# Hybrid HGRN2 / gMLP trunk on one core: conditioning's small transfers on ScalarE's queue, a new sequence of its work, and rows of x scaled on ScalarE

## The chip, the cores and the metric

One Trainium2 chip, one core. The metric is device time in microseconds of one execution. Engines: TensorE (PE, its weight loads PEld), VectorE (DVE), ScalarE (ACT), GpSimd (POOL) and SyncE (SP), which issues most of the transfers. An engine executes its instructions in the order in which they stand in its queue.

## The reference

One layer over 2048 latent positions of width 1024, with a context of 256 positions. Cut to what the change touches:

```python
ada   = silu(c)     @ w_ada + b_ada        # (1024) @ (1024, 6144)
ada_c = silu(c_ctx) @ w_ada + b_ada
hc = modulate(rmsnorm(ctx, norm_mix), csh1, csc1)    # y * (1 + scale) + shift
... = hgrn2_gates(hc @ w_in[:, :3 * 512], ...)       # the context's final states
h  = modulate(rmsnorm(x, norm_mix), sh1, sc1)
... = token_mixers(h @ w_in, ...)                    # recurrence and spatial gating on x
x = x + g1 * (o @ w_out)
x = x + g2 * conv_ffn(modulate(rmsnorm(x, norm_ffn), sh2, sc2), ...)
return rmsnorm(x, norm_final)
```

All data are float32. The large products are made from two parts of each factor: a high part that the matmul reads at full rate and a low part that holds the rest (hi·hi, hi·lo, lo·hi).

## The kernel before, in words

The part that the change touches is the first some 400 us of the program.

**Conditioning** stands in a block whose order is written out by hand, lines 299 to 358: each engine gets its instructions in the order of the lines. `cs2` holds silu of `c` and of `c_ctx`. Of `w_ada`'s 512 columns at a time ("groups" 0 to 3: two of shifts, two of scales), each group is loaded in two 1 MB halves on SyncE's queue. For groups 0, 2 and 3 TensorE multiplies (`ada_products`, 4 k-blocks per half), the result is added to a row of `b_ada` in a tile `rows` (`load_bias`), and four small transposes and two small copies bring it into columns (`ada_columns`, `put_ada`). Group 1 is made on VectorE: `ada_sums(k0, k1)` adds two products of 128x512 for each k into `acc`, whose first partition was loaded with `b_ada`; 16 small matmuls against `ones` then make columns of it (`pz`).

The two context tiles `xc` are squared on ScalarE (`x_square`), the root is made on POOL (`rstd`), VectorE scales them in place (`x_scale`), and TensorE transposes them into four PSUM banks (`pct`). `ctx_mod(k, eng)` turns a k-block into high and low parts: VectorE applies scale and shift (line 231, into `xfl`, two buffers), ScalarE copies the high part (line 119), and the engine `eng` subtracts to get the low part (line 120). `split_w` does the same to a weight tile of 128x1024 (`whi`, `wlo`).

**Context banks.** `run_banks` goes through banks of 256 columns, 24 matmuls each, for heads' gates and values; each needs its weight split (two sets of `whi`, `wlo`; a set is free when its bank is done). The first uses weight columns 0, the second 512, the third 1024.

**The x stage.** After the hand-written block an automatic scheduler orders each engine's instructions. `pin` puts an instruction behind all that was written before it on its engine. `bg_q` holds work that is interleaved with the banks: `x_start` squares four rows of x tiles, makes the root, scales them (`x_scale`), and `x_first` transposes them per k and calls `x_mod` (the same three steps as `ctx_mod`, 128x512); then the next four. Low parts alternate: POOL for even k, VectorE for odd k. `x_second` does the second half of x in four groups of two, 256 columns at a time, with 6 us planned between loading, scaling and use, and writes the parts to DRAM.

Small transfers: the six rows of `vr` (norm gains and the like) are issued by ScalarE; the rows of `b_ada` by SyncE, between the large loads.

Of the kernel before, what the change touches and what calls it, by code (L numbers as in the profile page):

```python
# [13 lines left out]
AF = mybir.ActivationFunctionType  # L14
ALU = mybir.AluOpType
# [4 lines left out]
D = 1024  # L20
# [4 lines left out]
CTX = 256  # L25
HW = 512
# [46 lines left out]
def tile_trunk(ctx, tc, x, c, cx, c_ctx, w_ada, b_ada, norm_mix, norm_ffn, w_in, hg_norm, sgu_g, sgu_b,  # L73
               w_sp, b_sp, w_out, w_up, conv_w, conv_b, w_down, norm_final, masks, out):
    nc = tc.nc
    V, S, G, T = nc.vector, nc.scalar, nc.gpsimd, Tensor(nc.tensor)
    ld = nc.sync.dma_start
# [31 lines left out]
    def rstd(pool, ss, n, scale, bias=EPS, keep=lambda i: i):  # L109

        r = pool.tile([P, 8], F32, tag="rs", name="rs")
        keep(G.tensor_scalar(out=r[:, :n], in0=ss, scalar1=scale, scalar2=bias, op0=ALU.mult, op1=ALU.add))  # L112
        r2 = pool.tile([P, 8], F32, tag="rs2", name="rs2")
        G.tensor_tensor(out=r2[:, :n], in0=r[:, :n], in1=mhalf[:, :n], op=ALU.pow)  # L114
        return r2
# [61 lines left out]
    with es1:  # L177
# [21 lines left out]
        def load_raw(key):  # L199
            raw = raw_tile().rearrange("p (k c) -> p k c", c=P)  # L200
            ld(raw, w_in[:, key[0]:key[0] + P].rearrange("(k p) c -> p k c", p=P))
            w_raw[key] = raw
# [16 lines left out]
                jk = pm.tile([P, D], BF16, tag="acc", name="xjk")  # L219
                keep(S.activation(jk, xt, AF.Square, accum_out=ss[:, i0 + i:i0 + i + 1]))  # L220

        def x_scale(xs, ss, keep=pin):

            r = rstd(pm, ss[:, :len(xs)], len(xs), 1.0 / D, keep=keep)
            for i, xt in enumerate(xs):
                keep(V.tensor_scalar(out=xt, in0=xt, scalar1=r[:, i:i + 1], scalar2=None, op0=ALU.mult))

        def x_mod(pt, which, k, hi, lo, n, eng):

# [21 lines left out]
        def load_ada(g, qs=(0, 1)):  # L251

            for q in (qs,) if isinstance(qs, int) else qs:
                t = wa[g // 2][:, 4 * (g % 2) + 2 * q:4 * (g % 2) + 2 * q + 2, :]
                wts[g, q] = t.rearrange("p a (b e) -> p (a b) e", e=512)
                ld(wts[g, q], wv[:, 4 * q:4 * q + 4, g * 512:(g + 1) * 512])

        def load_bias(g, tag):
            rows[g] = pm.tile([2, 512], F32, tag=tag, name="rows", bufs=2)
            ld(rows[g], b_ada[0:1, g * 512:(g + 1) * 512].broadcast_to([2, 512]))  # L260

        def ada_products(g, q):
            if q == 0:
                pa[g] = bank("pj")
            for k in range(4 * q, 4 * q + 4):
                T.matmul(pa[g][:2, :], cs2[:, k, :], wts[g, q][:, k % 4, :], start=(k == 0), stop=(k == 7))

        def ada_columns(g):
            V.tensor_add(rows[g], rows[g], pa.pop(g)[:2, :])
            pv = bank("pj")  # L270
            for j in range(4):
                T.transpose(pv[:, 2 * j:2 * j + 2], rows[g][:, j * P:(j + 1) * P], ident[:2, :2])
            put_ada(g, [pv[:, w:8:2] for w in range(2)])

        def ada_sums(k0, k1):
            for k in range(k0, k1):
                for w in range(2):
                    V.scalar_tensor_tensor(out=acc[:, w, :], in0=wts[1, k // 4][:, k % 4, :], scalar=cs2[:, k, w:w + 1],
                                           in1=acc[:, w, :], op0=ALU.mult, op1=ALU.add)
# [13 lines left out]
        def ctx_mod(k, eng):  # L293
            x_mod(pct[k // 2][:, (k % 2) * 256:(k % 2) * 256 + 256], 1, k, chl[:, k, :], cll[:, k, :], CTX, eng)
# [4 lines left out]
        with tc.manual_schedule():  # L299
            load_ada(2)  # L300
            for i in range(2):
                ld(xc[i], cx[0][i * P:(i + 1) * P, :])
            vr = pm.tile([50, P], F32, tag="gu", name="vr", bufs=2)
            for a, n, r0 in ((norm_mix[0], 8, 0), (norm_ffn[0], 8, 8), (hg_norm[0], 4, 16), (sgu_g[0], 4, 20),
                             (sgu_b[0], 4, 24), (conv_b[0], 22, 28)):
                S.dma_start(vr[r0:r0 + n, :], a.rearrange("(r p) -> r p", p=P))
            load_bias(2, "ot")
            for q in range(2):
                load_ada(0, q)
                load_ada(1, q)  # L310
            load_bias(0, "ot")
            for w in range(2):
                ld(acc[0:1, w, :], b_ada[0:1, 512:1024])
            load_bias(3, "vv")
            load_ada(3)
            load_raw((0, CTX))
            S.activation(sg, cc, AF.Sigmoid)
            V.tensor_mul(cs2.rearrange("p k w -> p w k"), cc, sg)
            ss = x_sums()
            x_square(xc, ss, keep=lambda i: i)  # L320
            ada_products(2, 0)
            pv = bank("sc")
            T.transpose(pv[:, :50], vr, ident[:50, :50])
            V.tensor_copy(vec, pv[:, :50])
            ada_products(2, 1)
            ada_columns(2)
            x_scale(xc, ss, keep=lambda i: i)
            ada_sums(0, 4)
            ada_products(0, 0)
            for k in range(NK):  # L330
                for i in range(2):
                    o = (k % 2) * 256 + i * P
                    T.transpose(pct[k // 2][:, o:o + P], xc[i][:, k * P:(k + 1) * P], ident)
            load_raw((HW, CTX))
            ada_products(0, 1)
            ada_columns(0)
            ada_sums(4, 5)
            for k in range(4):
                ctx_mod(k, G)
                if k == 1:  # L340
                    ada_sums(5, 6)
            ada_products(3, 0)
            load_raw((2 * HW, CTX))
            for i in range(4):
                ld(xg[i], x_rows[i])
            ada_sums(6, 8)
            nxt[0, CTX] = split_w((0, CTX), G)
            ada_products(3, 1)
            pz = bank("pj")
            for w in range(2):  # L350
                for j in range(4):
                    o = 2 * (4 * w + j)
                    T.matmul(pz[:, o:o + 2], acc[:, w, j * P:(j + 1) * P], ones[:, :2], start=True, stop=True)
            ada_columns(3)
            put_ada(1, [pz[:, 8 * w:8 * w + 8:2] for w in range(2)])
            for k in range(4, NK):
                ctx_mod(k, V)
            nxt[HW, CTX] = split_w((HW, CTX), V)
        xl = p1.tile([P, NK, TH], F32R, tag="xl", name="xl", align_bytes=AL)
        xh = p1.tile([P, NK, TH], F32R, tag="xh", name="xh", align_bytes=AL)  # L360

        def x_first(g0, xs):
            for k in range(NK):
                pt = bank("mi")
                for i in range(4):
                    pin(T.transpose(pt[:, i * P:(i + 1) * P], xs[i][:, k * P:(k + 1) * P], ident))
                sl = slice(g0 * P, g0 * P + 512)
                x_mod(pt, 0, k, xh[:, k, sl], xl[:, k, sl], 512, V if k % 2 else G)
                if k % 2:
                    yield 1.6  # L370

# [1234 lines left out]
```

## Time and profile before

| | us |
|---|---|
| median of 3 runs | 2584.08 |
| lowest, highest | 2579.35, 2584.96 |
| profiled execution, its own time | 2583.23 |
| its span, first to last instruction | 2581.3 |
| TensorE busy / VectorE / POOL / ScalarE | 2503.6 / 1634.9 / 1052.7 / 905.0 |
| mean granted TensorE clock | 0.992 |

A line of the timeline reads: start, duration, engine, line, operation, output<-inputs, shapes, count, and in brackets how long the engine stood idle before it and what ended that. "ACTq" and "SPq" are the issues of transfers by ScalarE and SyncE. A row of the busy time by stretches gives the stretch, its length, each engine's busy time with its count of instructions, the granted TensorE clock (1.00 is full), the share of the DMA engines, and GB/s. "L231" is line 231 of the kernel before.

### The profile page before, as it was taken

How to read it: one execution, taken by the hardware profiler on the slowest of the kernel's cores; microseconds unless marked ns; L12 is line 12 of the kernel's file. 1: busy time of each engine (PE TensorE's matmuls, PEld its weight loads, DVE VectorE, ACT ScalarE, POOL GpSimd, SP SyncE). 2: the span in 40 equal slices, each digit the busy share in tenths (PEclk: the TensorE clock that was granted, in tenths of full speed). 3: DMA queues.
4: the chain of work that ended last, by engine and by line, in shares of the span. 5: the costliest groups of instructions: out<-in, count | busy, mean ns of one | idle time of the engine just before them, and what ended most of it. 6: DMA issues, size and time to landing. Idle time of an engine off the chain costs nothing. (4 is left out here: it accounts for less than half of the span.)

```text
span 2581.3 us, 32786 instructions
## 1 busy us (share of the span) xinstructions
PE 2503.6 (97%) x12123; PEld 2066.2 (80%) x12123; DVE 1634.9 (63%) x2174; ACT 905.0 (35%) x1524; POOL 1052.7 (41%) x871
## 2 busy tenths in 40 slices
PE   7999999999999998999999999999999999999997
PEld 4787887888888887788788888788788888888886
DVE  5867784644555666466898778599999983212212
ACT  2554334333434332344433333333333332111111
POOL 1344232232243243002687887877877810000000
PEclk8999999999999999999999999999999999999999
DMA  8355445561022124668722222732222364313221
GB/s 286 105 193 163 145 123 196 184 209 58 30 86 82 43 84 163 212 208 273 243 88 95 77 92 89 268 125 90 88 89 89 101 204 128 114 45 114 73 90 67
DMA packets 282492, 336.42 MB, mean 130 GB/s; under 512 B 31057, under 2 KB 214089, under 8 KB 278621
## 3 DMA queue, kind: packets, MB, share of 16 engines
q1 hardware_dynamic: 279076, 333.59, 39.2%
q8 instruction: 96, 1.57, 0.2%
q10 hardware_dynamic: 3257, 0.75, 0.1%
q14 instruction: 63, 0.52, 0.1%
HBM read 236.69 MB, written 97.59 MB: 129 GB/s over the span
## 5 line engine op out<-in xcount | busy, mean ns | idle before, releaser
L1281 DVE SCALAR_TENSOR_TENSOR dn<-gp,taps,dn 128x1024 f32<-128x1024 f32 x352 | 448.0, 1279 | 20.6 <-ACT dn L1278 17.3
L120 POOL TENSOR_TENSOR Al<-raw,Ah 128x512 fp32r<-128x512 f32 x264 | 344.8, 1314 | 96.2 <-ACT Ah L119 88.4
L65 PE MATMUL pj<-xh,whi 128*128 128x512 f32 x896 | 364.9, 408 | 0.5 <-ACT xh L119 0.5
L65 PE MATMUL pj<-xl,whi 128*128 128x512 f32 x896 | 351.9, 393 | 1.8 <-DVE xl L120 1.1
L65 PE MATMUL pj<-xh,wlo 128*128 128x512 f32 x896 | 352.2, 393 | 1.0 <-DVE wlo L120 1.0
L65 PE MATMUL up<-xah,Al 128*128 128x512 f32 x704 | 275.8, 392 | 2.3 <-POOL Al L120 2.3
L65 PE MATMUL up<-xah,Ah 128*128 128x512 f32 x704 | 276.3, 393 | 1.7 <-ACT Ah L119 1.7
L65 PE MATMUL up<-yl,Ah 128*128 128x512 f32 x704 | 274.3, 390 | 3.2 <-DMA yl<-yd 3.1
L112 POOL TENSOR_SCALAR rs<-ss 128x1 f32<-128x1 f32 (+1 forms) x24 | 7.1, 297 | 642.0 <-DVE xt L1516 323.3
L119 ACT CAST Ah<-raw 128x512 fp32r<-128x512 f32 x265 | 161.1, 618 | 299.2 <-PE up L65 249.4
L120 DVE TENSOR_TENSOR ml<-mr,mh 128x512 fp32r<-128x512 f32 x85 | 58.7, 690 | 299.7 <-ACT mh L119 299.7
L120 POOL TENSOR_TENSOR wlo<-raw,whi 128x1024 fp32r<-128x1024 f32 x56 | 140.8, 2514 | 230.9 <-ACT whi L119 215.6
L65 PE MATMUL up<-yh,Ah 128*128 128x512 f32 x528 | 208.1, 395 | 0.0
L65 PE MATMUL up<-yh,Al 128*128 128x512 f32 x528 | 206.9, 392 | 0.0
L65 PE MATMUL up<-xal,Ah 128*128 128x512 f32 x528 | 205.5, 389 | 0.0
L65 PEld LDWEIGHTS pj<-xh,wlo 128*128 128x128 f32 x896 | 169.0, 189 | 37.3 <-DVE wlo L120 1.7
L65 PEld LDWEIGHTS pj<-xh,whi 128*128 128x128 f32 x896 | 169.6, 189 | 34.3 <-issue 3.5
L65 PEld LDWEIGHTS pj<-xl,whi 128*128 128x128 f32 x896 | 169.6, 189 | 33.5 <-DVE xl L120 2.1
L65 PE MATMUL dn<-wo,o 128*128 128x512 f32 x768 | 184.9, 397 | 3.7 <-DMA wo<-wo_d 2.2
L65 PE MATMUL dn<-wh,ml 128*128 128x512 f32 x480 | 186.8, 389 | 0.0
L65 PE MATMUL dn<-wl,mh 128*128 128x512 f32 x480 | 186.8, 389 | 0.0
L65 PE MATMUL dn<-wh,mh 128*128 128x512 f32 x480 | 186.7, 389 | 0.0
(307 smaller groups left out, 4941.2 us busy)
## 6 DMA issues: line engine op xcount, KB each, us to landing
raw<-in_w_up_dram SPq DMA_DIRECT2D x88, 512.0 KB
raw<-in_w_in_dram SPq DMA_DIRECT2D x68, 512.0 KB
mr<-m SPq DMA_DIRECT2D x85, 256.0 KB
raw<-in_w_ada_dram SPq DMA_DIRECT2D x32, 512.0 KB
m<-cv SPq DMA_DIRECT2D x22, 544.0 KB
m<-cv SPq DMA_DIRECT2D x22, 480.0 KB
xt<-in_w_down_dram SPq DMA_DIRECT2D x19, 512.0 KB
wa<-in_w_ada_dram SPq DMA_DIRECT2D x8, 1024.0 KB
```

Source lines behind the costliest of these rows:

```text
L65: return self.engine.matmul(out, lhsT, rhs, **kw)
L112: keep(G.tensor_scalar(out=r[:, :n], in0=ss, scalar1=scale, scalar2=bias, op0=ALU.mult, op1=ALU.add))
L119: keep(S.copy(hi, raw))
L120: (eng or G).tensor_sub(lo, raw, hi.bitcast(F32))
L1281: V.scalar_tensor_tensor(out=cr, in0=gt[:, t // 3:t // 3 + RH, t % 3:t % 3 + GW], scalar=taps[:, t * NF + f:t * NF + f + 1], in1=cr, op0=A ...
```

## The change

Four things change.

1. The rows of `b_ada` (three of `rows`, two of `acc`) are issued by ScalarE, behind the rows of `vr`, all of them ahead of the sigmoid on ScalarE. In the text SyncE's large loads now come first.
2. Conditioning's sequence is new: the addition of `b_ada` is a step of its own (`ada_rows`); the first half of group 0 comes before the columns of group 2; ten of the sums follow, then the transposes, group 0's second half and columns, both halves of group 3, the other six sums, and then the context's parts; `split_w` of the first two weights runs on POOL and stands ahead of parts 0 and 2; parts 0 to 3 have their low part on VectorE, 4 and 6 on POOL, 5 and 7 on VectorE.
3. `x_scale` scales rows of x on ScalarE (Identity with a scale per partition). The context's two tiles are still scaled on VectorE.
4. In `x_first` all low parts are made on POOL.

```diff
-        def x_scale(xs, ss, keep=pin):
+        def x_scale(xs, ss):
-            r = rstd(pm, ss[:, :len(xs)], len(xs), 1.0 / D, keep=keep)
+            r = rstd(pm, ss[:, :len(xs)], len(xs), 1.0 / D, keep=pin)
             for i, xt in enumerate(xs):
-                keep(V.tensor_scalar(out=xt, in0=xt, scalar1=r[:, i:i + 1], scalar2=None, op0=ALU.mult))
+                pin(S.activation(xt, xt, AF.Identity, scale=r[:, i:i + 1]))
...
         def load_bias(g, tag):
             rows[g] = pm.tile([2, 512], F32, tag=tag, name="rows", bufs=2)
-            ld(rows[g], b_ada[0:1, g * 512:(g + 1) * 512].broadcast_to([2, 512]))
+            S.dma_start(rows[g], b_ada[0:1, g * 512:(g + 1) * 512].broadcast_to([2, 512]))
...
+        def ada_rows(g):
+            V.tensor_add(rows[g], rows[g], pa.pop(g)[:2, :])
+
         def ada_columns(g):
-            V.tensor_add(rows[g], rows[g], pa.pop(g)[:2, :])
             pv = bank("pj")
...
             load_ada(2)
             for i in range(2):
                 ld(xc[i], cx[0][i * P:(i + 1) * P, :])
+            for q in range(2):
+                load_ada(0, q)
+                load_ada(1, q)
+            load_ada(3)
+            load_raw((0, CTX))
             vr = pm.tile([50, P], F32, tag="gu", name="vr", bufs=2)
...
                 S.dma_start(vr[r0:r0 + n, :], a.rearrange("(r p) -> r p", p=P))
-            load_bias(2, "ot")
-            for q in range(2):
-                load_ada(0, q)
-                load_ada(1, q)
-            load_bias(0, "ot")
+            for g, tag in ((2, "ot"), (0, "ot"), (3, "vv")):
+                load_bias(g, tag)
             for w in range(2):
-                ld(acc[0:1, w, :], b_ada[0:1, 512:1024])
-            load_bias(3, "vv")
-            load_ada(3)
-            load_raw((0, CTX))
+                S.dma_start(acc[0:1, w, :], b_ada[0:1, 512:1024])
             S.activation(sg, cc, AF.Sigmoid)
...
             ada_products(2, 1)
+            ada_rows(2)
+            r = rstd(pm, ss[:, :2], 2, 1.0 / D)
+            for i in range(2):
+                V.tensor_scalar(out=xc[i], in0=xc[i], scalar1=r[:, i:i + 1], scalar2=None, op0=ALU.mult)
+            ada_products(0, 0)
             ada_columns(2)
-            x_scale(xc, ss, keep=lambda i: i)
-            ada_sums(0, 4)
-            ada_products(0, 0)
+            ada_sums(0, 5)
...
             load_raw((HW, CTX))
-            ada_products(0, 1)
-            ada_columns(0)
-            ada_sums(4, 5)
-            for k in range(4):
-                ctx_mod(k, G)
-                if k == 1:
-                    ada_sums(5, 6)
-            ada_products(3, 0)
             load_raw((2 * HW, CTX))
             for i in range(4):
                 ld(xg[i], x_rows[i])
-            ada_sums(6, 8)
+            ada_products(0, 1)
+            ada_rows(0)
+            ada_columns(0)
+            ada_products(3, 0)
+            ada_sums(5, 8)
+            ada_products(3, 1)
             nxt[0, CTX] = split_w((0, CTX), G)
-            ada_products(3, 1)
+            ctx_mod(0, V)
+            ctx_mod(1, V)
+            nxt[HW, CTX] = split_w((HW, CTX), G)
+            ctx_mod(2, V)
+            ctx_mod(3, V)
+            ada_rows(3)
             pz = bank("pj")
...
+            put_ada(1, [pz[:, 8 * w:8 * w + 8:2] for w in range(2)])
             ada_columns(3)
-            put_ada(1, [pz[:, 8 * w:8 * w + 8:2] for w in range(2)])
             for k in range(4, NK):
-                ctx_mod(k, V)
-            nxt[HW, CTX] = split_w((HW, CTX), V)
+                ctx_mod(k, V if k % 2 else G)
...
-                x_mod(pt, 0, k, xh[:, k, sl], xl[:, k, sl], 512, V if k % 2 else G)
+                x_mod(pt, 0, k, xh[:, k, sl], xl[:, k, sl], 512, G)
```

## The prediction

> **What bounds the kernel now.** I read the page's head first, then the busy time by stretches, then the timeline of the first 90 us, then the waits of the DMA queue's own engine.
>
> ```profile
> span 2581.3 us, 32786 instructions
> PE 2503.6 (97%) x12123; PEld 2066.2 (80%) x12123; DVE 1634.9 (63%) x2174; ACT 905.0 (35%) x1524; POOL 1052.7 (41%) x871
> ...
> core 0: us, PE busy (x) PEld busy (x) DVE busy (x) ACT busy (x) POOL busy (x), PEclk, DMA share, GB/s
> 7.00:43.50 36.50, 29.81 (x93) 10.27 (x93) 19.88 (x30) 4.87 (x9) 7.84 (x7) 0.93 1.04 380
> 43.50:55.70 12.20, 10.88 (x50) 9.60 (x51) 6.44 (x14) 6.24 (x12) 0.00 (x0) 0.66 0.34 110
> 64.70:87.00 22.30, 19.00 (x126) 15.72 (x125) 20.69 (x30) 13.00 (x24) 12.68 (x7) 1.00 0.33 95
> 87.00:105.00 18.00, 16.24 (x91) 12.43 (x90) 16.79 (x30) 7.61 (x15) 5.64 (x4) 1.00 0.26 88
> 105.00:400.00 295.00, 286.61 (x1576) 241.65 (x1576) 216.16 (x340) 125.54 (x203) 107.57 (x82) 0.99 0.49 155
> ```
>
> TensorE is busy for 97% of the span, and the change takes no matmul out. It can win or lose only where TensorE stands idle, or runs at half clock, up to about 400 us: conditioning (to 43.5), the first context banks (to 55.7), and the stage that normalises x (to 105), where VectorE is busy for 20.69 of 22.30 us while TensorE loses 3.3. After 105 us the idle is 8.4 of 295. Now the order inside conditioning:
>
> ```profile
> 6.98 5.45 PE L65 MATMUL pj<-wa,cs 128*2 128x512 f32 x8 [6.98 <-DMA wa<-in_w_ada_dram]
> 12.55 3.60 PE L65 MATMUL pj<-wa,cs 128*2 128x512 f32 x8
> 22.59 5.39 DVE L278 SCALAR_TENSOR_TENSOR acc<-wa,cs,acc 128x512 f32<-128x512 f32 x8 [3.68 <-DMA acc<-in_b_ada_dram]
> 27.90 0.67 DVE L269 TENSOR_TENSOR rows<-rows,pj 2x512 f32<-2x512 f32 x1
> ...
> 29.07 0.23 DVE L285 COPY s<-pj 128x4 f32<-128x4 f32 x2 [0.50 <-PE pj L69]
> ...
> 34.40 5.71 DVE L278 SCALAR_TENSOR_TENSOR acc<-wa,cs,acc 128x512 f32<-128x512 f32 x4
> 36.11 2.78 POOL L120 TENSOR_TENSOR wlo<-raw,whi 128x1024 fp32r<-128x1024 f32 x1
> 39.55 3.54 PE L65 MATMUL pj<-ones,acc 128*128 128x2 f32 x16 [3.56 <-POOL wlo L120]
> 43.54 0.58 PE L65 MATMUL pj<-ch,whi 128*128 128x256 f32 x1
> 44.12 0.55 DVE L231 TENSOR_SCALAR xfl<-mi,a,s 128x256 f32<-128x256 f32 x1
> 49.19 0.43 DVE L120 TENSOR_TENSOR cl<-xfl,ch 128x256 fp32r<-128x256 f32 x1 [0.47 <-ACT ch L119]
> 51.42 0.39 PE L65 MATMUL pj<-ch,wlo 128*128 128x256 f32 x1 [0.76 <-DVE wlo L120]
> ```
>
> VectorE's sums for group 1 (line 278) wait at 22.59 for a 2 KB row of b_ada that stood behind the megabyte loads on SyncE's queue. They end at 34.40 + 5.71 = 40.1, and TensorE's context banks start behind them, at 43.54. The first bank crawls behind parts 4 to 7 of the context, which end at 49.62. The second waits for its weight's low part until 51.42.
>
> **Part 1, conditioning.** One more reading of the timeline is needed here, of what POOL and VectorE do to each other:
>
> ```profile
> 118.82 2.48 POOL L120 TENSOR_TENSOR wlo<-raw,whi 128x1024 fp32r<-128x1024 f32 x1 [1.21 <-ACT whi L119]
> 118.98 2.60 DVE L469 TENSOR_TENSOR cS<-cS,tot 128x256 f32<-128x256 f32 x1
> 121.70 0.42 DVE L469 TENSOR_TENSOR cS<-cS,tot 128x256 f32<-128x256 f32 x1
> ```
>
> A VectorE piece over two SBUF tiles that meets one of POOL's lasts until POOL is done (2.60 us instead of 0.42).
>
> The row of b_ada comes early, so the sums can start when VectorE comes to them. In the new order that is after the columns of group 2, which TensorE makes only after the first half of group 0. That half has 8 matmuls like the 3.60 us row: 12.55 + 3.60 + 3.60 = 19.75, and the columns follow the rows by 29.30 - 28.57 = 0.73 today, which gives 20.5. Ten sums at 5.39 / 8 = 0.67 end at 27.2, and the rows of group 0 follow; today they start at 27.90, with eight sums done and not ten. The other six start at about 28.7 and end at 32.7 clean. Here POOL's low part of the first weight falls into them; today four sums beside such a piece took 5.71 and not 2.7, so 35.7 if it costs as much. Then four context parts wholly on VectorE: today four take 49.62 - 44.12 = 5.5, so 38.2 to 41.2. The second weight's low part now runs on POOL beside them; it costs nothing, or up to the 2.4 us of such a piece on POOL (2.48 at 118.82). So 38.2 to 43.6, and with 0.67 for the rows of group 3 and some 0.5 for their transposes the first bank starts at 39.4 to 44.8 against 43.54. Parts 4 to 7 alternate POOL and VectorE: 5.3 instead of 6.1 us, since one engine's low part overlaps the other's next part. The first bank's end moves by -4.9 to +0.5 us. I take -2.3, the middle, because both collisions have a row but neither is certain to hit in full. The second bank no longer waits for its low part; that 1.3 us is hidden by the next paragraph's chain.
>
> The clock is the second cost in this stretch.
>
> ```profile
> 36.00:38.00 2.00, 0.00 (x0) 1.00 1.01 408
> 40.00:42.00 2.00, 2.00 (x11) 0.50 0.84 235
> ```
>
> TensorE idle from 36 had half its clock by 40. In the new order it stands idle while VectorE does the four context parts, so the first bank starts at half clock again. I book no change. The Trainium skill, page "TensorE: Matmul & The Clock Gate", section "Part 1: The HAM clock gate (the "warmup" mystery)", says that an idle window of about 3.4 us halves the clock and that a busy one restores it. The halving after 36 agrees; by that rule a longer wait ahead of the first bank would cost up to one more such window at half rate, 1.7 us by an estimate from that page, and the sum would be nearer to zero.
>
> **Part 2, rows of x on ScalarE.**
>
> ```profile
> 58.40 1.06 ACT L220 ACTIVATE xjk<-xg 128x1024 bf16<-128x1024 f32 x1
> 59.99 1.06 POOL L114 TENSOR_TENSOR rs<-rs,mhalf 128x4 f32<-128x4 f32 x1
> 61.09 2.74 DVE L226 TENSOR_SCALAR xg<-xg,rs 128x1024 f32<-128x1024 f32 x4 [0.91 <-POOL rs L114]
> 63.88 0.76 PE L69 MATMUL mi<-ident,xg 128*128 128x128 f32 x5 [0.33 <-DVE xg L226]
> 66.41 3.38 POOL L120 TENSOR_TENSOR xl<-xfl,xh 128x512 fp32r<-128x512 f32 x1 [5.36 <-ACT xh L119]
> 67.59 0.68 DVE L120 TENSOR_TENSOR xl<-xfl,xh 128x512 fp32r<-128x512 f32 x1
> 71.37 1.29 POOL L120 TENSOR_TENSOR xl<-xfl,xh 128x512 fp32r<-128x512 f32 x1 [1.58 <-ACT xh L119]
> ```
>
> Squares of x's first four rows, POOL's root and the scaling are one chain, and TensorE stands at its end (63.88, waiting for xg). The squares sit on ScalarE behind the first bank's gates, so the chain moves with that bank: -2.3. The trace has no scaling on ScalarE; the nearest row is the square over the same 128x1024, 1.06 us. Four make 4.24 in place of 2.74, so this group's transposes end 1.5 us later in the chain. What waits behind the scaling on ScalarE is the next weight's cast; in exchange VectorE reaches that weight's low part 2.74 sooner, so I count no more than the 1.5. Net at this barrier: -2.3 + 1.5 = -0.8, from -3.4 to +2.0. The chain is thus the wait that takes the place of the old one: most of the gain of conditioning ends here.
>
> **Part 3, low parts of x on POOL.** Of 16 low parts eight move from VectorE (0.68) to POOL (1.29 clean, 3.38 when VectorE's own pieces come between). VectorE is rid of 8 x 0.68 = 5.4 and, with the two groups' scaling, 5.5 us more in a stage where it binds. TensorE's idle there is 3.3 + 1.8 = 5.1 us, which is the ceiling of the gain. Against it stands that POOL's extra 8 x 1.29 = 10.3 us hold VectorE: as the piece at 118.98 shows. If half of POOL's 10.3 us held VectorE, half of the 10.9 would be left. I take a quarter of the ceiling, -1.3: half of the relief is left, and of the waits that it could shorten about half hang on ScalarE's casts too. The ends are -4 (nearly the ceiling) and +4 (each of the two groups' last parts, now one behind the other on POOL, late by 2 us).
>
> **Part 4, the second half of x** (four groups of two rows between 105 and 400 us): eight scalings leave VectorE, eight come to ScalarE, 43% busy there. Its pieces have 6 us of planned distance to their users. I take 0, from -1.5 to +2.
>
> Sum: -0.8 - 1.3 + 0 = -2.1 us. The profiled execution took 2583.23 (2581.3 of span and 1.9 around it), 0.85 below the median of 2584.08. From the median: **2582.0**. The terms' ends add to -8.9 and +8.
>
> **The rivals.**
>
> A, the gain holds: TensorE has other banks to run while ScalarE scales, and the collisions of part 1 miss. Then -4.9 from conditioning and -2.5 from the x stage: 2576.7, about 2577. For it: VectorE's load in 64.7 to 87. Against: 58.40 to 63.88 is a chain that no faster VectorE shortens.
>
> B, slower: ScalarE's queue holds up the sigmoid.
>
> ```profile
> SPq L302 <- DMA vr<-in_norm_ffn_dram: 0.2, 1, 0.2
> ...
> 2.70 0.30 ACTq L306 DMA_DIRECT2D vr<-in_conv_b_dram  x1
> 3.29 1.28 ACT L317 ACT_TABLE_LOAD   x1 [3.29 <-DMA cc<-in_c_ctx_dram]
> 4.84 0.17 DVE L318 TENSOR_TENSOR cs<-cc,sg 128x16 f32<-128x16 f32 x1 [4.84 <-ACT sg L317]
> 12.09 1.06 ACT L220 ACTIVATE xjk<-raw 128x1024 bf16<-128x1024 f32 x1 [0.18 <-DMA raw<-in_ctx_dram]
> ```
>
> Six issues of about 0.3 us become eleven, ahead of the sigmoid: cs at 4.84 + 1.5 = 6.4, still under the 6.98 at which the first weights land, so hidden with 0.6 to spare. But the first row matters: the load of ctx (line 302) waited for an unrelated row of vr to land before it could be issued. If one of the five new issues waits like that for a big load, everything on ScalarE stands behind it, the sigmoid first, then all products. From a landing at about 8 us on it costs time; if it is the second ctx tile's (12.09), cs comes at 12.09 + 0.5 + 1.28 + 0.4 = 14.3, 7.3 us behind 6.98: 2582 + 7.3, about 2589.5.
>
> C, slower: POOL becomes the bound of the x stage. If the low parts all take 3.38, eight need 27 us where the first group's stretch has 22.3 and the second's 18: some 5 to 9 us on 2582: about 2589.
>
> D, the transfers don't overtake, and the row of b_ada lands at 22.59 as now. Ten sums then end at 29.3 and the rows of group 0 come 2.1 us late: 2582 + 2.1, about 2584. The Trainium skill, page "DMA: Bandwidth & Descriptors", section "Issuing engines are not separate DMA queues", says that another issuing engine saves only the issue time, since all run on the same 16 engines. No row here shows a small ScalarE transfer among large ones.
>
> **How the numbers follow.** A measurement of this kernel tells about 0.2% (5.2 us) from no change; its three runs span 5.6 us. The forecast, 2582, has 0.40, D 0.07: within 0.2%, 0.47. A has 0.30: faster. B has 0.15 and C 0.08: slower, 0.23. The range reaches from 2572 (the terms' low ends with the whole of A's first term, -10.4, and a little for the order of later work) to 2592 (the high ends, +8, and B and C).
>
> **What would show it.** Right: acc lands well before 20 us, sums start near 20.5 and end by 36, the second bank follows the first without a wait for wlo, and the transposes of xg wait for ScalarE's scaling instead, near 63. POOL's low parts average over 1.3 us. Wrong: sums still starting at 22.6 (D); the sigmoid after 7 us with a DMA issue just ahead of it (B); xg's first transposes before 60 us, with the stretch to 105 shorter by over 4 us (A); a row "PE waits for POOL xl" of several us (C). A difference that arises after 400 us would refute the whole account, since nothing of the change lies there.

## The result, and the profile after

| | before | after |
|---|---|---|
| median, us (5 runs each) | 2582.16 | 2592.78 |
| lowest, highest | 2579.35, 2584.96 | 2589.64, 2596.15 |
| ratio after/before, 95% interval | | 1.0039 [1.0025, 1.0053] |
| span of the profiled execution | 2581.3 | 2589.2 |

The change made the kernel slower by 10 us. (The prediction started from the median of the first three runs of before, 2584.08; with five it is 2582.16.) The head of the page after, and the busy time by the stretches that the prediction showed:

```profile
span 2589.2 us, 32777 instructions
PE 2507.6 (97%) x12123; PEld 2068.5 (80%) x12123; DVE 1616.4 (62%) x2151; ACT 920.7 (36%) x1540; POOL 1060.4 (41%) x878
```

```profile
7.00:43.50 36.50, 30.14 (x89) 8.54 (x89) 21.05 (x33) 7.01 (x12) 5.67 (x4) 0.93 1.04 371
43.50:55.70 12.20, 9.95 (x68) 9.67 (x69) 6.44 (x15) 6.06 (x14) 1.48 (x2) 0.79 0.36 121
64.70:87.00 22.30, 17.41 (x112) 14.50 (x111) 10.55 (x11) 17.81 (x30) 15.86 (x11) 0.98 0.19 57
87.00:105.00 18.00, 15.26 (x85) 11.76 (x83) 12.22 (x17) 7.31 (x16) 8.62 (x6) 0.93 0.34 110
```

VectorE was relieved as the change says: in 64.7 to 87 it is busy for 10.55 us instead of 20.69. TensorE, the engine that counts, did less there, 17.41 us instead of 19.00, and in the next stretch ran at a clock of 0.93 instead of 1.00. An engine that looked like the bound was freed, and TensorE gained nothing by it.

Where the time goes is read by following the same matmul through the traces. Each number is the start of that matmul against the kernel before, in us (positive is later); "hi·hi 16" is the 16th product of x's high part with a weight's high part, eight to a bank. The columns are the kernel after and four kernels of the experiments below.

| matmul (its start before) | after | conditioning alone | x stage alone | low parts alone | second half alone |
|---|---|---|---|---|---|
| first product of conditioning (6.98) | +2.1 | +2.3 | +0.2 | +0.2 | +0.2 |
| first context bank (43.54) | +2.0 | +1.7 | -0.5 | -1.4 | -0.1 |
| third context bank (55.65) | -2.9 | -1.8 | -0.5 | -1.4 | -1.6 |
| hi·hi 8 (83.21) | -2.1 | +1.9 | -2.7 | -2.3 | -1.6 |
| hi·hi 16 (97.41) | +6.0 | +7.5 | +5.3 | +5.7 | -1.6 |
| hi·hi 80 (169.13) | +4.6 | +5.9 | +3.8 | +5.4 | -2.8 |
| hi·hi 128 (214.23) | +8.1 | +5.2 | +10.1 | +5.7 | +3.5 |
| end (2581.35) | +7.9 | +0.4 | +9.1 | +4.7 | +0.3 |

Up to 115 us "second half alone" has the instructions of the kernel before in the same order on every engine, and still stands 1.6 us ahead at 56 us: single executions differ by that much, and what is smaller is not read from one trace. The medians decide on totals.

So the kernel after starts 2 us late, is 3 us ahead at the third context bank, loses 8 us between hi·hi 8 and 16 (83 to 103 us), and 3.5 us between hi·hi 80 and 128. After 215 us nothing is added in these traces.

**The start.** Timeline of the kernel after, ScalarE, VectorE and TensorE:

```profile
3.06 0.88 ACTq L260 DMA_DIRECT2D rows<-in_b_ada_dram  x3
5.43 1.84 ACTq L317 DMA_DIRECT2D acc<-in_b_ada_dram  x2
7.30 1.28 ACT L318 ACT_TABLE_LOAD   x1 [7.30 <-DMA rows<-in_b_ada_dram]
8.60 0.22 ACT L318 ACTIVATE sg<-cc 128x16 f32<-128x16 f32 x1
...
8.84 0.18 DVE L319 TENSOR_TENSOR cs<-cc,sg 128x16 f32<-128x16 f32 x1 [8.84 <-DMA wa<-in_w_ada_dram]
...
9.08 4.42 PE L65 MATMUL pj<-wa,cs 128*2 128x512 f32 x5 [9.08 <-DVE cs L319]
```

The three issues of `rows` end at 3.94; the two of `acc` take 0.23 us each and yet stretch from 5.43 to 7.27. ScalarE's queue stood still twice, and the sigmoid behind it came at 8.60. The trace keeps, with each issue, the semaphore that it waits for. The first issue of `acc` waits for number 106, and the transfer that signals 106 is the row of `vr` that ScalarE issued at 2.00; the second waits for number 100, signalled by the row of `vr` issued at 2.71. The program gives the same few semaphore numbers to one transfer after another, so an issue stands until an unrelated small row has landed, here until 5.4 and 7.0 us.

**The x stage.** The same view at 79 to 98 us:

```profile
79.25 2.53 POOL L120 TENSOR_TENSOR xl<-xfl,xh 128x512 fp32r<-128x512 f32 x2 [1.18 <-ACT xh L119]
81.86 0.19 POOL L112 TENSOR_SCALAR rs<-xss 128x4 f32<-128x4 f32 x1
82.14 1.01 POOL L114 TENSOR_TENSOR rs<-rs,mhalf 128x4 f32<-128x4 f32 x1
83.11 2.35 POOL L120 TENSOR_TENSOR wlo<-raw,whi 128x1024 fp32r<-128x1024 f32 x1
...
83.18 4.27 ACT L226 ACTIVATE xk<-xk,rs 128x1024 f32<-128x1024 f32 x4 [2.53 <-POOL rs L114]
...
85.52 0.39 PE L65 MATMUL pj<-ch,wlo 128*128 128x256 f32 x1 [2.72 <-POOL wlo L120]
...
90.48 1.53 DVE L231 TENSOR_SCALAR xfl<-mi,a,s 128x512 f32<-128x512 f32 x2 [11.57 <-PE mi L69]
...
97.03 0.50 PE L65 MATMUL pj<-xl,whi 128*128 128x512 f32 x1 [1.23 <-POOL xl L120]
```

On POOL one queue holds the low parts of x, then the root for the next four rows, then the eighth weight's low part (`wlo`). TensorE has run out of other banks and waits 2.72 us for the last of these, ScalarE waits for the middle one, and VectorE, relieved, stands idle for 11.57 us. In the kernel before, the same low part of the eighth weight stood ahead of the root on POOL:

```profile
77.00 2.38 POOL L120 TENSOR_TENSOR wlo<-raw,whi 128x1024 fp32r<-128x1024 f32 x1
...
81.58 1.06 POOL L114 TENSOR_TENSOR rs<-rs,mhalf 128x4 f32<-128x4 f32 x1
...
83.80 2.74 DVE L226 TENSOR_SCALAR xk<-xk,rs 128x1024 f32<-128x1024 f32 x4
```

What the wait costs beyond itself is in the busy time by stretches, after first and then before:

```profile
82.00:84.00 2.00, 0.80 (x4) 0.51 (x4) 0.00 (x0) 0.82 (x1) 1.92 (x3) 1.00 0.00 0
84.00:86.00 2.00, 0.48 (x4) 0.48 (x5) 0.00 (x0) 2.00 (x3) 1.46 (x1) 1.00 0.00 0
86.00:88.00 2.00, 2.00 (x13) 2.00 (x12) 0.00 (x0) 2.00 (x4) 0.00 (x0) 0.55 0.62 178
88.00:90.00 2.00, 2.00 (x13) 2.00 (x13) 0.00 (x0) 0.18 (x1) 0.00 (x0) 0.59 0.28 85
```

```profile
82.00:86.00 4.00, 3.72 (x22) 2.84 (x22) 3.31 (x6) 1.38 (x3) 0.65 (x1) 1.00 0.11 32
86.00:90.00 4.00, 3.99 (x35) 3.69 (x33) 2.51 (x5) 1.50 (x4) 1.28 (x1) 1.00 0.02 4
```

In these 8 us TensorE before works 7.71 us at full clock. After, it works 0.80 + 0.48, and then 2.00 x 0.55 + 2.00 x 0.59: 3.6 us of full clock, 4.1 less. Of that, 1.7 us (2.00 x 0.45 + 2.00 x 0.41) is the clock alone. The rest of the 8 us follows in the second group, where TensorE waits for `xl` on POOL four times between 93 and 103 us, 2.6 us in all; what makes the last 1.4 us was not separated.

**The second half of x** (timeline after, 175 to 184 us):

```profile
175.72 2.19 ACT L226 ACTIVATE xk<-xk,rs 128x1024 f32<-128x1024 f32 x2 [1.28 <-POOL rs L114]
...
179.72 1.04 ACT L119 CAST whi<-raw 128x1024 fp32r<-128x1024 f32 x1
...
181.15 2.33 POOL L120 TENSOR_TENSOR wlo<-raw,whi 128x1024 fp32r<-128x1024 f32 x1
...
183.53 0.39 PE L65 MATMUL pj<-ch,wlo 128*128 128x256 f32 x1 [2.22 <-POOL wlo L120]
```

ScalarE waits for POOL's root with the scaling at the head of its queue; the next weight's cast stands behind it (and behind a table load and an activation that before came after the cast) and ends at 180.8, and its low part on POOL at 183.5. Before, the low part was done at 173.4, 3.3 us ahead of its first use:

```profile
169.78 1.05 ACT L119 CAST whi<-raw 128x1024 fp32r<-128x1024 f32 x1 [0.67 <-PE pj L65]
170.91 2.47 POOL L120 TENSOR_TENSOR wlo<-raw,whi 128x1024 fp32r<-128x1024 f32 x1 [0.58 <-ACT whi L119]
...
176.69 0.28 PE L65 MATMUL pj<-ch,wlo 128*128 128x256 f32 x1
```

### The profile page after: what moved, and what is told of

It is laid out like the page before. It is cut to its first block, busy times and chain, and to the rows that moved or that the text cites. A ratio compares the mean times of both kernels' runs of the same rounds, so it can differ in the third digit from the quotient of the medians.

```text
span 2589.2 us, 32777 instructions
## 1 busy us (share of the span) xinstructions
PE 2507.6 (97%) x12123; PEld 2068.5 (80%) x12123; DVE 1616.4 (62%) x2151; ACT 920.7 (36%) x1540; POOL 1060.4 (41%) x878
```

## The experiments

Ratios are to the kernel before, from runs on the same chip, with 95% intervals. Expectations speak of "x banks" 79, 95 and 127 and mean single hi·hi products counted from 0; their "second x bank (97.4 us)" is the row "hi·hi 16" above.

### One part taken back

Scaling of x's rows on VectorE again, the rest as after:

```
-                pin(S.activation(xt, xt, AF.Identity, scale=r[:, i:i + 1]))
+                pin(V.tensor_scalar(out=xt, in0=xt, scalar1=r[:, i:i + 1], scalar2=None, op0=ALU.mult))
```

> The changed kernel with rows of x scaled on VectorE again; all else as changed. Theory S (ScalarE's scaling costs the time: 4.27 us against 2.74 for a group of four rows, and the second group's transposes wait for it at half clock): 5 to 8 us come back, about 2586, and the second group's first xfl starts near 87 instead of 90.5. Theory P (POOL's queue costs it: root and the eighth weight's low part stand behind eight low parts of x): at most 2 us come back, about 2591, and the wait for that low part, 2.7 us at 85.5, stays.

1.0039 [1.0027, 1.0052]: nothing comes back. That is the total of theory P, but the wait that P names is gone from the trace, and another stands there: VectorE's four scalings now meet POOL's low part of the eighth weight, take 4.81 us, and TensorE waits 3.81 us for them, so that hi·hi 16 stands at +10.8. The loss of the second half, in turn, is gone (+10.2 at hi·hi 80, +9.5 at 128).

Low parts of the first half alternating again:

```
-                x_mod(pt, 0, k, xh[:, k, sl], xl[:, k, sl], 512, G)
+                x_mod(pt, 0, k, xh[:, k, sl], xl[:, k, sl], 512, V if k % 2 else G)
```

> The changed kernel with the low parts of x's first half alternating between POOL and VectorE again; all else as changed. Theory P (POOL's queue): 5 to 8 us come back, about 2586, the 2.7 us wait of TensorE near 85 goes, and the half clock behind it. Theory S (ScalarE's scaling): at most 2 us come back, about 2591.

1.0034 [1.0022, 1.0045]. In the trace hi·hi 16 stands 2.3 us behind the kernel before instead of 6.0, so that loss is gone, but between hi·hi 80 and 96 it loses 4.5 us (from +1.8 to +6.3), and the total is within the uncertainty of the kernel after. The 5 to 8 us that theory P promised did not come back.

Both taken back, which leaves the new conditioning alone:

> The changed kernel with both reverted, so only the new conditioning and ScalarE's transfers are left. If the x stage (scaling and low parts together) holds the loss: 2580 to 2584, equal to before within 2 us, though its first context bank starts about 2 us later than before's 43.5. If conditioning with the sigmoid behind ScalarE's transfers holds it: 2588 to 2593.

1.0014 [1.0005, 1.0022], between the two totals that were expected. Alone it loses, too, although its third bank is 1.8 us early: 3.7 us up to hi·hi 8, for which see below, and 5.6 us from there to hi·hi 16, where the scaling meets POOL's low part of the eighth weight as in the first run:

```profile
85.94 2.34 POOL L120 TENSOR_TENSOR wlo<-raw,whi 128x1024 fp32r<-128x1024 f32 x1
86.00 4.81 DVE L226 TENSOR_SCALAR xk<-xk,rs 128x1024 f32<-128x1024 f32 x4 [1.18 <-POOL rs L114]
...
88.97 0.45 PE L69 MATMUL mi<-ident,xk 128*128 128x128 f32 x1 [3.26 <-DVE xk L226]
```

The x stage alone (the kernel before with both edits of the x stage):

> The kernel before with only the x stage changed (rows of x scaled on ScalarE, low parts of the first half on POOL), conditioning untouched. If the x stage holds the loss: 2589 to 2593. If conditioning holds it: 2581 to 2585.

1.0039 [1.0027, 1.0052]: the whole loss, without conditioning. Its timeline shows the 2.71 us wait for the eighth weight's low part and the 2.22 us wait of the second half, as after.

The sigmoid and `cs2` put ahead of the five b_ada transfers, the rest as after:

```
+            S.activation(sg, cc, AF.Sigmoid)
+            V.tensor_mul(cs2.rearrange("p k w -> p w k"), cc, sg)
             for g, tag in ((2, "ot"), (0, "ot"), (3, "vv")):
                 load_bias(g, tag)
...
-            S.activation(sg, cc, AF.Sigmoid)
-            V.tensor_mul(cs2.rearrange("p k w -> p w k"), cc, sg)
```

> The changed kernel with the sigmoid of c and the product cs2 placed ahead of the five b_ada transfers on ScalarE's queue. Theory (the loss is made in the x stage; the late sigmoid is a small matter of its own): cs2 back at about 4.9 us, first product at 7.0 instead of 9.1, first context bank 1 to 2 us earlier than in the changed kernel (45.5), but the wait for the eighth weight's low part and those for xl in the second group remain, so at the second x bank at most 2 us of the 8 come back: 2591, ratio 1.003 to 1.004. Rival (the late sigmoid shifts the whole chain and so makes the collisions): the x stage falls back into step, 2584 or less.

1.0029 [1.0018, 1.0039]. The first product is back at 6.9 us, 1.4 us of the 6.0 come back at hi·hi 16, and the total is near the theory's. The waits that the theory names do not stay where they were, though: at 82.03 TensorE waits 2.17 us for the scaled rows and not for the eighth weight's low part, and at 95.19 it waits 2.50 us for VectorE's `xfl`.

### The stall at 85 us, and the second half

The eighth weight's low part on VectorE:

```
-            split(hi, lo, raw, eng or (V if w_n[0] < 8 or w_n[0] < 20 and w_n[0] % 2 else G))
+            split(hi, lo, raw, eng or (V if w_n[0] < 9 or w_n[0] < 20 and w_n[0] % 2 else G))
```

> The changed kernel with the eighth weight's low part on VectorE instead of POOL, nothing else. Theory (the stall at 85.5 us is POOL's queue: that weight's low part stands behind the serial low parts of x and the root, TensorE waits 2.72 us and then runs 3 us at half clock): the wait shrinks to under 1 us, the second x bank comes 3 to 5 us earlier than in the changed kernel (103.4 us), the total is 2588 to 2590. Rival (the stall is set by ScalarE's scaling or by the second group's xl on POOL, and would only move): the wait reappears at xk or xl, second x bank within 1.5 us of the changed kernel's, 2592 to 2593.

1.0038 [1.0025, 1.0052]; hi·hi 16 at +6.7. Timeline:

```profile
85.09 4.27 ACT L226 ACTIVATE xk<-xk,rs 128x1024 f32<-128x1024 f32 x4 [3.41 <-POOL rs L114]
...
86.29 0.33 PE L69 MATMUL mi<-ident,xk 128*128 128x128 f32 x1 [2.44 <-ACT xk L226]
```

The rival holds in the trace: the wait of 2.72 us for `wlo` became one of 2.44 us for the scaled rows, which wait for POOL's root. The total, 2591.6, lies between the two expected, no different from the kernel after's.

The second half of x scaled on VectorE, the first half on ScalarE, the rest as after:

> The changed kernel with the rows of the second half of x (four groups of two) scaled on VectorE again; the first half's on ScalarE as changed. Theory (two scalings of 1.1 us on ScalarE, which also wait for POOL's root, stand ahead of the next weight's cast, so that its low part reaches TensorE late at 183.5 us, 2.2 us of idle and a lower clock behind it): no wait for wlo near 183, the 3.5 us between the x banks 79 and 127 come back, 2588 to 2590. Rival (that loss belongs to the order of later work, shifted by what came before): the loss of 3 to 4 us between those banks remains, 2592 to 2593.

1.0033 [1.0022, 1.0045], 2590.4 us. The step of 3.5 us between hi·hi 80 and 128 is gone from the trace (+7.1 to +6.4, no wait for `wlo` near 183 us). The ratio falls by 0.0006, some 1.5 us, which cannot be told from nothing. So what makes this step is shown; what it is worth in the total is not.

### Each edit of the x stage alone, on the kernel before

> The kernel before with one thing changed: the 16 low parts of the first half of x all on POOL. Theory (POOL's queue makes the loss at the second x bank: the low parts stand one behind the other, the root of the second four rows and the eighth weight's low part behind them): the second x bank comes 5 to 8 us later than before (97.4 us), total 2586 to 2591. Rival (the prediction's step: VectorE is relieved where it binds): second x bank 1 to 4 us earlier, total 2578 to 2581.

1.0024 [1.0014, 1.0035]; 8.0 us lost between hi·hi 8 and 16. Timeline, and busy time by stretches:

```profile
81.61 1.01 POOL L114 TENSOR_TENSOR rs<-rs,mhalf 128x4 f32<-128x4 f32 x1
82.59 2.34 POOL L120 TENSOR_TENSOR wlo<-raw,whi 128x1024 fp32r<-128x1024 f32 x1
...
82.65 4.81 DVE L226 TENSOR_SCALAR xk<-xk,rs 128x1024 f32<-128x1024 f32 x4 [3.74 <-POOL rs L114]
...
85.62 0.45 PE L69 MATMUL mi<-ident,xk 128*128 128x128 f32 x1 [3.59 <-DVE xk L226]
```

```profile
82.00:86.00 4.00, 0.41 (x3) 0.41 (x3) 3.35 (x2) 0.00 (x0) 2.93 (x2) 0.84 0.00 0
86.00:90.00 4.00, 4.00 (x21) 4.00 (x20) 1.94 (x4) 0.00 (x0) 0.00 (x0) 0.50 0.45 131
```

Four scalings that met POOL's low part took 4.81 us, not 2.74, and TensorE stood nearly still for 4 us and then ran at half clock for 4 more. The theory holds at hi·hi 16 and in the total.

> The kernel before with one thing changed: the rows of the second half of x scaled on ScalarE. Theory (the scaling stands ahead of the next weight's cast on ScalarE while it waits for POOL's root): nothing before 160 us; between the x banks 79 and 95 (169 to 186 us) 3 to 5 us lost, with a wait of TensorE for wlo of about 2 us; total 2585 to 2588. Rival (the prediction's step: six microseconds of planned distance cover it): within 2 us of the kernel before, 2580 to 2584.

1.0023 [1.0014, 1.0032]. The same wait of 2.22 us for `wlo` (at 177.23), a clock of 0.72 in the 6 us behind it, and 5.0 us lost between hi·hi 80 and 96. The prediction's "0" for this part is refuted.

> The kernel before with one thing changed: both groups of the first half of x scaled on ScalarE, low parts alternating as before. Theory (with POOL not serial, ScalarE's scaling is cheap here): first transposes of x 1.3 us later, as in the kernel with the x stage alone, second x bank 0 to 2 us later, total 2581 to 2584. Rival (ScalarE's scaling holds up the casts in the second group by 4.3 us): second x bank 4 us or more later, 2586 to 2588.

1.0021 [1.0012, 1.0031], 2587.3 us. Hi·hi 16 stands 1.7 us late, as the theory says, but the total is the rival's. The trace puts 2.4 us before 120 us and 3 us in the feed-forward part after 1000 us, where the change has no instruction; where this part's loss arises stays open.

Then the low parts alone once more, with the eighth weight's low part on VectorE (the edit as above):

> The kernel before with the 16 low parts of the first half of x on POOL (as in the run with the low parts alone, 1.0024) and the eighth weight's low part on VectorE instead of POOL. In the run with the low parts alone VectorE's scaling of the second four rows took 4.81 us instead of 2.74, beside POOL's low part of that weight, and TensorE waited 3.59 us for it. Theory (half of the loss is that collision, the other half that TensorE has run out of other banks by then): the scaling takes 2.7 to 3.0 us, the wait at the transposes of xk shrinks to 1 to 2 us, total 2583 to 2586. Rival (the place of that weight does not matter, the serial low parts of the second group make the loss): second x bank still 5 us or more behind the kernel before, total 2587 to 2589.

1.0020 [1.0011, 1.0030], hi·hi 16 at +6.1. Busy time by stretches:

```profile
86.00:90.00 4.00, 3.81 (x21) 3.52 (x21) 3.24 (x5) 0.54 (x2) 0.00 (x0) 0.60 0.26 78
...
94.00:98.00 4.00, 2.02 (x11) 1.39 (x9) 3.93 (x7) 2.44 (x5) 1.91 (x2) 1.00 0.00 0
98.00:102.00 4.00, 3.63 (x13) 2.94 (x14) 4.00 (x7) 1.24 (x2) 2.71 (x2) 0.68 0.54 178
```

The collision is gone (the scaling takes 2.74 us, TensorE waits 1.52 us for it), but the loss stays: a second gap of 2.34 us ends at 98.37, with a second fall of the clock. TensorE waits there for VectorE's `xfl`, which starts at 97.51 behind other work: VectorE is busy for 3.93 of the 4 us before 98. It had come late to that work, after waiting 1.55 us for POOL's `xl` before another `xfl`, and two of its pieces met POOL's low parts (1.13 and 1.40 us; such pieces take 0.43 alone). At hi·hi 16 the rival holds, and the total is just under its range: the loss does not hang on this one collision. How much of it comes of the low parts standing one behind the other on POOL, and how much of the other order of VectorE's work, is not separated.

The second half on ScalarE (against the run with that alone) with 3 us between squares and scaling:

```
                 x_square(xs, ss)
+                yield 3.0
                 x_scale(xs, ss, on_act=True)
-                yield 6.0
+                yield 3.0
```

> The kernel before with the rows of the second half of x scaled on ScalarE (as in the run with that alone, 1.0023), and 3 us of planned distance put between the squares and the scaling (taken from the 6 us behind it), so that the scheduler puts the next weight's cast ahead of the scaling on ScalarE. Theory (the loss is that cast standing behind a scaling that waits for POOL's root): no wait of TensorE for wlo near 177 us, total 2581 to 2585. Rival (ScalarE's 1.1 us a row against VectorE's 0.75 is itself the loss, or another wait takes its place): 2586 to 2588.

1.0028 [1.0017, 1.0039]. The wait for `wlo` is gone; at 207.18 TensorE waits instead for the scaled rows:

```profile
207.18 0.48 PE L69 MATMUL mi<-ident,xk 128*128 128x128 f32 x1 [6.46 <-ACT xk L227]
```

The rival holds: another wait takes its place.

### Conditioning, and a version that beats both

The new conditioning alone, with the sigmoid ahead:

> The new conditioning alone (x stage as before), with the sigmoid and cs2 ahead of the b_ada transfers on ScalarE's queue. Theory (the late first product accounts for 2 us of the 4.4 that the new conditioning alone costs; the rest is lost at the fourth context bank, where the squares of x's first rows stand ahead of the weights' casts on ScalarE): first bank 1 to 2 us before the kernel before's, total 2583 to 2585. Rival (an earlier start only lengthens the wait at the fourth bank): 2586 to 2587. A total under 2580 would make it the version that beats both.

0.9984 [0.9975, 0.9993], 2577.1 us: faster than both kernels, and more than either side expected. One edit of place on ScalarE's queue is worth 0.0030 here, some 8 us, where the first product moves by 2.3. TensorE's waits, in the timeline of conditioning alone and then of this kernel:

```profile
58.96 0.39 PE L65 MATMUL pj<-ch,whi 128*128 128x256 f32 x1 [1.00 <-ACT whi L119]
60.88 0.39 PE L65 MATMUL pj<-ch,wlo 128*128 128x256 f32 x1 [1.41 <-DVE wlo L120]
62.82 0.48 PE L69 MATMUL mi<-ident,xg 128*128 128x128 f32 x1 [0.88 <-DVE xg L226]
```

```profile
54.67 0.38 PE L65 MATMUL pj<-ch,whi 128*128 128x256 f32 x1 [0.72 <-ACT whi L119]
56.19 0.58 PE L65 MATMUL pj<-ch,wlo 128*128 128x256 f32 x1 [1.02 <-DVE wlo L120]
...
81.33 0.30 PE L69 MATMUL mi<-ident,xk 128*128 128x128 f32 x1 [0.92 <-DVE xk L226]
```

Conditioning alone has three waits in the fourth context bank, after which TensorE's clock is 0.50 from 62 to 66 us. The kernel with the sigmoid ahead has two there, shorter ones, and its clock is 0.78 and 0.80 from 54 to 62 us. The larger difference comes later: TensorE waits 0.92 us for the scaled rows at 81.33 and not 3.26, because POOL makes the eighth weight's low part at 70.83, ahead of the root, and the four scalings take 2.74 us. But the automatic scheduler also ordered the later work otherwise in the two, some weights' casts and squares of x on ScalarE among it. The next run keeps the order of conditioning alone and takes away one of the two late issues:

```
-            for w in range(2):
-                S.dma_start(acc[0:1, w, :], b_ada[0:1, 512:1024])
+            acc_in = b_ada[0:1, 512:1024].rearrange("o (a e) -> o a e", a=1)
+            S.dma_start(acc[0:1, :, :], acc_in.broadcast_to([1, 2, 512]))
```

> The new conditioning alone with the two transfers of b_ada's row into acc made into one; the sigmoid stays behind the transfers on ScalarE's queue, and every engine's later order of instructions is that of the new conditioning alone (2586.3), which the kernel with the sigmoid ahead (2577.1) does not share: there the scheduler placed some casts of weights and squares of x otherwise. Theory (the 9 us between those two are mostly the late first product, which later waits and the half clock multiply): cs comes at about 7.4 instead of 9.0 us, the first product at 7.5, and most of the difference goes: 2578 to 2581. Rival (the 9 us are mostly the scheduler's other order): only the 1.6 us of the start come back or less, 2584 to 2586.

1.0011 [1.0003, 1.0020]. The first product comes at 8.11 instead of 9.27. From the third bank to the end of the x stage all stands 2.6 to 3.1 us earlier than in conditioning alone, but every wait is still there, in the fourth bank 0.99, 1.41 and 0.68 us, and for the scaled rows:

```profile
85.92 0.35 PE L69 MATMUL mi<-ident,xk 128*128 128x128 f32 x1 [3.25 <-DVE xk L226]
```

So the rival holds for the larger part: half of the delay taken away brought 0.0003 of the ratio, 0.8 us, within the uncertainty, though 2.6 to 3.1 us in the trace. The wait of 3.25 us does not hang on that half of the delay, and in the scheduler's other order it is 0.92. How much of the rest the last 1.1 us of delay is worth was not separated.

Two mixtures on top of it. With the first half of x scaled on ScalarE (low parts alternating, second half on VectorE):

> New conditioning with the sigmoid ahead of the b_ada transfers, first half of x scaled on ScalarE, its low parts alternating between VectorE and POOL, second half of x scaled on VectorE. Theory (three separate causes, each removed here: late sigmoid 2 us, low parts serial on POOL, ScalarE's scaling in the second half 5 to 6 us): the second x bank at most 1 us behind the kernel before (97.4 us), the total 2578 to 2583. Rival (the new order loses to the old one wherever it is put, since gains of conditioning end at the chain of x's first rows): 2585 to 2590.

1.0002 [0.9993, 1.0011]: no different from the kernel before, in the theory's range, but hi·hi 16 stands at +2.7 and not within 1 us. And with only the first four rows on ScalarE:

> The mixed kernel (new conditioning, sigmoid ahead of the b_ada transfers, low parts alternating, second half scaled on VectorE), but of the first half only the first four rows scaled on ScalarE and the second four on VectorE, which stood idle for 7.45 us at 79 to 86 us in the mixed kernel. Theory (the clock there, 0.84 at 80 to 88 us, and the second x bank, 2.7 us behind the kernel before, come of the 4.27 us of scaling on ScalarE): second x bank 1 to 3 us earlier than in the mixed kernel, total 2578 to 2581, faster than both. Rival (the order that the scheduler makes of it gives it back): 2581 to 2584.

1.0017 [1.0008, 1.0026], behind both theories. Its profiled execution, 2580.7 us, was the fastest of its eleven (median 2585.8), so its trace does not show where the median's loss lies; that stays open. Against the best kernel it loses 0.0033 with four scalings moved to ScalarE, and the mixture before it only 0.0018 with all eight: this is no price per scaling. One thing that the trace does show is the collision, since here the second four rows are scaled on VectorE: 4.85 us beside POOL's low part of the eighth weight at 79.09.

**What the traces share.** In the kernel before and in the best kernel POOL makes the eighth weight's low part ahead of the root, and the four scalings on VectorE take 2.74 us. In five others (scaling taken back, conditioning alone, that with one `acc`, low parts alone, the last mixture) it stands just behind the root, and they take 4.81 to 4.85. Moved to VectorE instead, that piece changed nothing measurable (1.0039 to 1.0038, and 1.0024 to 1.0020 with the low parts alone). No run puts it ahead of the root and leaves the rest, so what its place costs is not measured by itself.

## Why the prediction was wrong, by its steps

| part | forecast, us | alone: ratio x 2582 |
|---|---|---|
| 1, conditioning | -2.3 (-4.9 to +0.5) | +3.6 [+1.3, +5.7] |
| 2, first half's rows on ScalarE | +1.5 in the chain | +5.4 [+3.1, +8.0] |
| 3, low parts on POOL | -1.3 (-4 to +4) | +6.2 [+3.6, +9.0] |
| 4, second half on ScalarE | 0 (-1.5 to +2) | +5.9 [+3.6, +8.3] |
| x stage in all | | +10.1 [+7.0, +13.4] |

The four add to 21, the change cost 10: they share waits, and where one edit is taken back another wait takes the place of the one that goes. That is also why taking back one edit brought nothing measurable.

**Part 3 is the step that failed most.** It booked POOL's extra work as a load on VectorE (the collision at 118.98) and the relief of VectorE as the gain. The order in POOL's queue was not looked at: that the root of the next four rows and a weight's low part stand behind the low parts, and that TensorE, without other banks, waits at that place: 2.72 us, with 3.6 us of full clock done in the 8 us around it where before it was 7.71. Its high end, "late by 2 us" for each group, was the right kind of delay, and the clock behind it was left out. POOL's low parts averaged 1.27 to 1.76 us, so rival C's price (3.38 each) was wrong; its direction, and its row "PE waits for POOL xl", came true, in small waits and not in several microseconds.

**Part 2** was near its 1.5 us in the trace of that part alone, 1.7 at hi·hi 16; where the rest of its total comes from stays open.

**Part 4** took the planned distance of 6 us as cover for the user of the rows. It held for the rows: TensorE's waits for them were under a microsecond. It did not hold for what stood behind the scaling on ScalarE's own queue, a weight's cast, for whose low part TensorE waited 2.22 us. The prediction had named just that cast in part 2 and counted it at nothing.

**Part 1** was right in its first steps. (The middle of its range is -2.2; -2.3 was written.) With the sigmoid ahead, conditioning alone has its third bank 4.7 us early and gains 4 us in all. "Sums start near 20.5" came out at 23.04, 0.15 us after the columns of group 2 had begun to be taken up (22.89) and not behind a transfer; 2.1 of the 2.5 us are the late first product, and with the sigmoid ahead the sums start at 20.66, in the kernel after with that edit at 20.20. The late first product was rival B, whose mechanism came true at a third of its price: the second `acc` issue stood until 7.0 us, not until the second context tile, and what it stood for was a row of `vr`, not a big load. Rival D, transfers that do not overtake, is refuted by the same two starts: they come ahead of 22.59. What part 1 left out, and where it lost time alone by its trace, are the waits in the fourth bank and the collision at 86 us with TensorE's wait of 3.26 us for it.

**The clock** was booked as "no change" for the first stretch and not at all for the x stage. In the first stretch that held (0.93 and 0.93, and then 0.79 for 0.66). In the x stage no gap before had cost a clock: with waits of up to 1.06 us the clock was 1.00 throughout. After, one of 2.72 us cost 1.7 us more. Not every gap of that size has a price: the wait of 2.22 us at 183 us left the clock at 1.00 in the kernel after, and in the second half alone the same wait was followed by 0.72. The Trainium skill, page "TensorE: Matmul & The Clock Gate", section "Part 1: The HAM clock gate (the "warmup" mystery)", says that one idle window of about 3.4 us halves the clock. Here no full window without work was needed: in the run of the low parts with the eighth weight on VectorE no single wait from 90 to 98.4 us was over 2.34 us, TensorE was busy for 2.02 of the 4 us before 98, and the next four ran at 0.68.

**"A difference after 400 us would refute the account"**: in the trace after there is none, +7.8 us at 393 us and +7.9 at the end.

## What to carry to other kernels

An engine that is busy for nine tenths of a stretch need not be its bound: ask which queue the late instruction stands in, and list what stands behind each moved one on its new engine, the small root and the next weight's cast as much as the long pieces. A gap of 2 us or more on TensorE can bring half clock behind it, here up to as much again as the gap, and sometimes nothing. And where a scheduler orders the rest, an edit is one draw of a new order: try each part alone and in pairs, since here the best kernel was one part of the change with two lines moved.

## What the runs showed of the hardware beyond that

An issue of a small transfer can hold its engine for 1.4 us and more when its semaphore is still that of an earlier transfer: ScalarE's two issues of 0.23 us took from 3.94 to 7.27 us. The two small rows that they stood for took 3.4 and 4.3 us from their own issue (2.00 and 2.71) to the end of the wait.

A scaling on ScalarE takes 1.07 us for 128x1024 (four in 4.27), as the square did (1.06), and 0.69 on VectorE (four in 2.74). Next to a low part on POOL VectorE's four took 4.81. The Trainium skill, page "SBUF — State Buffer", section "Who interferes with whom", says that VectorE in a mode that uses two ports and POOL lock each other out for a whole instruction, and counts scaling by a scalar among the operations that can enter such a mode. The excess of 2.07 us beside a POOL piece of 2.34 agrees, and ScalarE's four, beside POOL pieces at 83.11 too, kept to 4.27.
